# Merging the triangular inverses of two heads in one block, and scaling the heads' outputs on ScalarE, in a bidirectional hybrid encoder layer

## The chip, the cores and the metric

The kernel runs on one core of a Trainium2 chip. The metric is the device time of one execution in microseconds (us), and "the time" of a kernel is the median of its runs. The core has five engines with a queue each: TensorE (PE in the profile; PEld is its weight load), VectorE (DVE), ScalarE (ACT), GpSimd (POOL) and SyncE (SP), which here issues transfers. Products are made by PE and land in PSUM, of which this kernel uses eight banks; all else lies in SBUF or in the chip's main memory.

## What is computed

One encoder layer on 512 positions of 1024 channels in float32: a feed-forward block, a token mixer, a second feed-forward block, a last norm. The change lies in the mixer, in its branch with a delta rule, which has 8 heads, chunks, and one scan per direction:

```python
k_beta = k * beta[..., None]
a_mat = jnp.where(strict, jnp.einsum('bhnid,bhnjd->bhnij', k_beta, k) * decay, 0.0)
a_mat = a_mat + jnp.eye(CHUNK, dtype=q.dtype)
sol = lax.linalg.triangular_solve(a_mat, rhs, left_side=True, lower=True)
...
o = _rmsnorm(o_fwd + o_bwd, dn_norm) * jax.nn.silu(dn_z.reshape(bn, s, DN_HEADS, DN_DV).astype(f32))
```

Instead of a solve the kernel forms the inverse of the unit triangular matrix (chunks of 128 positions, four per direction, so eight matrices of 128x128 for each head) and multiplies by it. The norm of the last line divides each row of a head's 512x128 output by its root mean square.

## The kernel before

Weights stream from main memory in tiles of 128 columns; each is split by ScalarE (`hi`, L219) and VectorE (`lo`, L221) in two halves, and three large products (L231 to L233, 128x128 by 128x512) replace one of full precision. The mixer makes 60 such projections. Between them stands the work of the heads, written as generators that are advanced step by step:

- `build` (`b0` to `b7`): short convolutions, the decays, and the strictly triangular matrices `nl` (L799) and the attention matrices `at` (L803). It transposes through banks tp and kq (L728).
- `invert` (`i0` to `i2`, one for each group of heads (0, 1, 2), (3, 4, 5), (6, 7)): the 32x32 diagonal blocks are inverted on VectorE, a chain of 60 small instructions (L829, L831), and written to main memory (`da`).
- `place` (`p0` to `p7`): four DMAs (L842) bring a head's 32x32 inverses to a pair of buffers `t64[i]` (i is the head's parity), and `merge` joins them in four stages, with a `yield` after each of the first three. Four transposes on VectorE (L851). First stage: 16 products of 32x32 (L858) in two banks, tp and kq, and two copies by ScalarE to `w` (L863). Second: 32 products (L869, L873) in the same two banks and four copies (L877, L879); this gives inverses of 64x64. Third: eight products of 64x64 (L885) in tp and a copy to `w2` (L887). Fourth: eight products (L891, L892) in tp; then VectorE (L905, L909) and GpSimd (L900 to L907) write the inverse with its factors over `nl`, as the factor `f`. A float32 product stands in the trace as two instructions.
- `scan` (`s0` to `s7`): four steps of both directions (products L923, L929, L940; ScalarE copies `y`, L932 and L934; VectorE `yw`, L937), the outputs (L952, L957, L960), then the norm: four squares with a sum on ScalarE (L968), two small VectorE instructions, a power on GpSimd (`rr`, L972), four multiplications by `rr` on VectorE (L974), one for each 128 positions, and four transposes by PE through bank tp (L979).

The order is a list written by hand, `EMIT`: each token advances one generator by one step. `advance` first completes what a step needs: `p` of a head needs `p` two heads earlier (they share `t64`) and its group's inverse; `s` needs `s` two heads earlier and its own `p`. Tokens `z`, `g`, `a`, `m`, `y` are projections and other work that depend on no scan step. From this order a scheduler at compile time makes each engine's fixed queue: among the instructions that it takes to be ready it chooses the earliest emitted. `keep_in_program_order` pins an instruction behind the one emitted before it on its engine; the first two stages' products are pinned, all but the first of each stage. Banks tp, kq and o have one buffer each, and PE's queue is worked in order.

## Time and profile before

| | |
|---|---|
| median of 3 runs | 1325.02 us (1324.39 to 1325.54) |
| profiled execution | 1323.76 us, of it the span 1321.6 us |
| PE busy | 1298.8 us (98%) |
| DVE, ACT, POOL busy | 960.6, 644.9, 64.4 us (73, 49, 5%) |
| mixer's merges and scans | from 540 to 872 us of the span |
| PE, DVE, ACT busy in these 332 us | 324.29, 229.82, 173.77 us |

The page of a profile gives each engine's busy time, the chain of work that ended last, and groups of instructions by line of the kernel. A group's row reads: line, engine, operation, what it writes and reads with sizes, count, busy time, mean nanoseconds of one, and the idle time of the engine just before these with what ended it. A row by line or tile has the minimum, median and maximum of one instruction in ns, and the first and last start. A row of the waits reads: who waited for whom, us in total, times, longest. A row in order of time reads: start, length, engine, line, operation; the ends of PE's products are modelled and overlap, so their starts tell the pace. A row of a stage reads: the stretch, its length, and the busy time of PE, PEld, DVE, ACT and POOL with the number of instructions, then PE's clock, the share of the DMA engines and GB/s.

### The profile page before, as it was taken

What the parts mean: (1) busy time and instruction counts of PE and PEld (TensorE: products, weight loads), DVE (VectorE), ACT (ScalarE), POOL (GpSimd) and SP (SyncE); (2) the same over time, 40 slices, a digit from 0 to 9 for tenths busy, and PEclk for the clock granted to TensorE, in tenths of its full rate; (3) what the DMA queues carried; (4) which work ended last, traced back from release to release, by engine and by line L of the source; (5) the groups of instructions that cost most, each with busy time, mean ns of one, the idle gap of its engine ahead of it and who ended that gap; (6) DMA issues with size and microseconds to landing.
All of it is one profiled execution on the core that took longest, in us unless ns stands there. A gap on an engine that the chain in (4) does not pass through costs nothing.

```text
span 1321.6 us, 22139 instructions
## 1 busy us (share of the span) xinstructions
PE 1298.8 (98%) x8489; PEld 1132.1 (86%) x8489; DVE 960.6 (73%) x1979; ACT 644.9 (49%) x1309; POOL 64.4 (5%) x104
## 2 busy tenths in 40 slices
PE   8999999999999999999999999999999999999997
PEld 7889998888898888787777787888999999998886
DVE  7968886777667889766956785648579888875442
ACT  4445563322357773566464334545446556653330
POOL 0000000000010110112012101000000000000000
PEclk9999999999999999999999999999999999999999
DMA  9433327898433543334333242667423323337421
GB/s 357 172 112 115 109 97 264 288 329 295 145 116 119 164 126 116 119 121 132 128 113 102 76 143 81 190 224 254 160 112 112 112 96 109 115 88 256 126 90 64
DMA packets 83026, 199.91 MB, mean 151 GB/s; under 512 B 25129, under 2 KB 27369, under 8 KB 82666
## 3 DMA queue, kind: packets, MB, share of 16 engines
q1 hardware_dynamic: 64984, 164.29, 37.4%
q10 hardware_dynamic: 17938, 34.23, 7.6%
q8 instruction: 66, 1.08, 0.3%
q14 instruction: 38, 0.31, 0.1%
HBM read 175.39 MB, written 23.10 MB: 150 GB/s over the span
## 4 chain that ended last, share of the span: by engine, by line
PE 82%; issue 9%; DVE 3%; ACT 2%; POOL 2%; DMA 1%; ACTq 0%; POOLq 0%; DVEq 0%; SPq 0%
PE acc L231 16%; PE acc L233 16%; PE acc L232 16%; PE acc L459 12%; PE ch L459 9%; PE acc L1215 1%; PE ch L929 1%; PE ch L1215 1%; PE o L952 1%; PE ch L940 1%; PE ch L957 1%; PE ch L923 1%; PE acc L1043 1%; PE acc L1041 1%; PE acc L1042 1%
## 5 line engine op out<-in xcount | busy, mean ns | idle before, releaser
L231 PE MATMUL acc<-uh,hi 128*128 128x512 f32 (+1 forms) x776 | 297.3, 385 | 0.6 <-DVE sps L644 0.5
L232 PE MATMUL acc<-uh,lo 128*128 128x512 f32 (+1 forms) x776 | 296.4, 383 | 0.1
L233 PE MATMUL acc<-ul,hi 128*128 128x512 f32 (+1 forms) x776 | 295.1, 382 | 0.0
L219 ACT CAST hi<-raw 128x512 fp32r<-128x512 f32 (+1 forms) x276 | 165.9, 612 | 262.9 <-PE acc L233 214.3
L221 DVE TENSOR_TENSOR lo<-raw,hi 128x512 fp32r<-128x512 f32 (+1 forms) x276 | 185.2, 680 | 136.6 <-ACT hi L219 135.0
L231 PEld LDWEIGHTS acc<-uh,hi 128*128 128x128 f32 x776 | 146.1, 189 | 24.8 <-issue 0.7
L232 PEld LDWEIGHTS acc<-uh,lo 128*128 128x128 f32 x776 | 146.0, 188 | 23.4 <-DVE lo L221 0.2
L233 PEld LDWEIGHTS acc<-ul,hi 128*128 128x128 f32 x776 | 145.5, 188 | 23.9
L231 PE MATMUL acc<-g,hi 128*128 128x512 f32 (+1 forms) x396 | 145.0, 366 | 0.0
L232 PE MATMUL acc<-g,lo 128*128 128x512 f32 (+1 forms) x396 | 144.5, 365 | 0.0
L233 PE MATMUL acc<-g,hi 128*128 128x512 f32 (+1 forms) x396 | 144.5, 365 | 0.0
L232 PEld LDWEIGHTS acc<-g,lo 128*128 128x128 f32 x396 | 74.4, 188 | 12.1
L233 PEld LDWEIGHTS acc<-g,hi 128*128 128x128 f32 x396 | 74.4, 188 | 12.0
L231 PEld LDWEIGHTS acc<-g,hi 128*128 128x128 f32 x396 | 74.4, 188 | 12.0
L459 PE MATMUL acc<-dh,hi 128*128 128x256 f32 x368 | 80.2, 282 | 0.0
L691 DVE SCALAR_TENSOR_TENSOR cacc<-acc,cvd_sb,cacc 128x510 f32<-128x510 f32 (+1 forms) x96 | 70.8, 741 | 2.5 <-ACT cacc L686 1.8
L242 DVE TENSOR_TENSOR lw<-raw,hw 128x1024 fp32r<-128x1024 f32 x42 | 51.4, 1224 | 28.8 <-ACT hw L241 28.2
L241 ACT CAST hi<-s 128x512 fp32r<-128x512 f32 x84 | 52.0, 619 | 34.3 <-PE ch L459 14.5
L241 ACT CAST hw<-raw 128x1024 fp32r<-128x1024 f32 x42 | 44.0, 1048 | 48.2 <-PE acc L459 26.7
L459 PE MATMUL acc<-dh,lo 128*128 128x256 f32 x224 | 63.3, 283 | 0.0
L459 PE MATMUL ch<-uh,lw 128*128 128x256 f32 x224 | 62.9, 281 | 0.0
L459 PE MATMUL ch<-ul,hw 128*128 128x256 f32 x224 | 62.8, 281 | 0.0
(385 smaller groups left out, 2812.0 us busy)
## 6 DMA issues: line engine op xcount, KB each, us to landing
raw<-w_in SPq DMA_DIRECT2D x60, 512.0 KB
room<-w_ada SPq DMA_DIRECT2D x40, 512.0 KB
raw<-w2u SPq DMA_DIRECT2D x35, 512.0 KB
raw<-w_ada SPq DMA_DIRECT2D x32, 512.0 KB
raw<-w1u SPq DMA_DIRECT2D x31, 512.0 KB
raw<-w1d SPq DMA_DIRECT2D x12, 512.0 KB
raw<-w2d SPq DMA_DIRECT2D x12, 512.0 KB
rb<-w2u SPq DMA_DIRECT2D x9, 512.0 KB
```

The lines of the kernel that those rows point to most:

```text
L219: act.copy(hi[:], raw[:, k : k + n, :])
L221: last["lo"] = dve.tensor_sub(lo[:], raw[:, k : k + n, :], hi[:].bitcast(F32))
L231: pe.matmul(ps[:, t0:t1], wh, rh[:, k0 + k, t0:t1], start=a, stop=False)
L232: pe.matmul(ps[:, t0:t1], wl, rh[:, k0 + k, t0:t1], start=False, stop=False)
L233: pe.matmul(ps[:, t0:t1], wh, rl[:, k0 + k, t0:t1], start=False, stop=b)
L241: act.copy(hi, src)
L242: dve.tensor_sub(lo, src, hi.bitcast(F32))
L459: pe.matmul(ps, a, b, start=first and k == 0 and a is wh and b is xh, stop=end, skip_group_check=not first)
L691: dve.scalar_tensor_tensor(out=acc[:, lo:hi], in0=src[:, lo + o : hi + o], scalar=w[:, i : i + 1], in1=acc[:, lo:hi], op0=ALU.mult, op1=AL ...
L923: pe.matmul(ps[:, 0:P], kT[:, c * P : c * P + P], S[:], start=True, stop=True)
L929: pe.matmul(ps[:, 0:P], f[:, n, :], r, start=True, stop=True)
L1215: pe.matmul(early[m][:], terms[i][0][:, m, :], terms[i][1], start=k == 0 and i == 0, stop=k == KT - 1 and i == 2)
```

## The change

Heads 0 and 1, 4 and 5, 6 and 7 are merged together; 2 and 3 stay alone. `LEADERS` sends every token of `p0`, `p4`, `p6` to `p1`, `p5`, `p7`, and the followers' tokens drop out of the order, so that a pair's stage stands where the leader's stood. `place` and `merge` take a list of heads. Per stage the products of the lower head come first, then the other's, in the same banks: bank columns 0 to 255 and 256 to 511 in the first, second and fourth stage, and a bank for each head (tp and kq) in the third. All stages' products are now pinned, all but the first of each. The copies keep their sizes and number, one set for each head, and follow all of the stage's products. In the last step VectorE's two multiplications are emitted ahead of GpSimd's. Apart from that, L974's multiplications become ScalarE activations (Copy with a factor for each row).

```diff
+LEADERS = {"p0": "p1", "p4": "p5", "p6": "p7"}
...
-            def place(i, s, da, j):
-                th, tht = t64[i]
-                for b in range(4):
...
-                return merge(s, t64[i])
+            def place(heads):
+
+                for i, s, da, j in heads:
+                    th, _ = t64[i % 2]
+                    for b in range(4):
...
+                return merge([(s, *t64[i % 2]) for i, s, _, _ in heads])
+
+            def pinned_products(todo):
+
+                for n, (out_, a, b) in enumerate(todo):
+                    x = pe.matmul(out_, a, b, start=True, stop=True)
+                    if n:
+                        tc.keep_in_program_order(x)
...
+                ps = [bank("tp", psx), bank("kq", psx)]
+                ws = [one.tile([P, 8, 32], F32, tag="w", bufs=2, name="w") for _ in heads]
+                pinned_products([(ps[b][a0 : a0 + 32, 256 * i + 32 * n : 256 * i + 32 * n + 32],
+                                  nls[i][d0 : d0 + 32, n, a0 : a0 + 32], heads[i][2][d0 : d0 + 32, n, 32:64])
+                                 for i in range(len(heads)) for n in range(8) for b, (a0, d0) in enumerate(halves)])
+                for i, w in enumerate(ws):
+                    for b, (a0, _) in enumerate(halves):
+                        act.copy(w[a0 : a0 + 32].rearrange("p a b -> p (a b)"),
+                                 ps[b][a0 : a0 + 32, 256 * i : 256 * i + 256])
                 yield
...
+                pinned_products(todo)
+                for i, (_, th, tht) in enumerate(heads):
+                    for b, (a0, d0) in enumerate(halves):
+                        o = slice(256 * i, 256 * i + 256)
+                        act.copy(tht[a0 : a0 + 32, :, 32:64], ps[b][a0 : a0 + 32, o].rearrange("p (a b) -> p a b", a=8))
+                        act.copy(th[d0 : d0 + 32, :, 0:32], ps[b][d0 : d0 + 32, o].rearrange("p (a b) -> p a b", a=8))
+                yield
+                ps = [bank(x, psx) for x in ("tp", "kq")[: len(heads)]]
+                pinned_products([(ps[i][0:64, 64 * n : 64 * n + 64], nls[i][64:128, n, 0:64], tht[64:128, n, :])
+                                 for i, (_, _, tht) in enumerate(heads) for n in range(8)])
...
-                for c in range(NC):
-                    dve.tensor_scalar(out=on[:, c, :], in0=on[:, c, :], scalar1=rr[:, 1, c : c + 1],
-                                      scalar2=None, op0=ALU.mult)
+                for c in range(NC):
+                    act.activation(out=on[:, c, :], in_=on[:, c, :], func=ACT.Copy, scale=rr[:, 1, c : c + 1])
...
             def done(t):
+                t = LEADERS.get(t, t)
                 return t in live and live[t] is None
...
-            for t in EMIT + [f"s{i}" for i in range(H)] * 20 + ["z", "g", "a", "m", "y"] * 20:
+            for t in [x for x in EMIT if x not in LEADERS] + [f"s{i}" for i in range(H)] * 20 + ["z", "g", "a", "m", "y"] * 20:
                 advance(t)
```

## The prediction

> **What bounds the kernel now.** I read the page first: its busy row, the slices, the shares of the chain.

> ```profile
> span 1321.6 us, 22139 instructions
> PE 1298.8 (98%) x8489; PEld 1132.1 (86%) x8489; DVE 960.6 (73%) x1979; ACT 644.9 (49%) x1309; POOL 64.4 (5%) x104
> ...
> PEclk9999999999999999999999999999999999999999
> ...
> PE 82%; issue 9%; DVE 3%; ACT 2%; POOL 2%; DMA 1%; ACTq 0%; POOLq 0%; DVEq 0%; SPq 0%
> ```

> TensorE (PE) is busy for 98% of the span at full clock and holds 82% of the chain. Time is therefore won only where PE issues less or stands less; time saved on another engine counts only if PE was waiting for it. The change touches the mixer's stretch in which heads are merged and scanned, so the second view is the busy time by stage, and the third, over the same stretch, whom PE waited for.

> ```profile
> 540.00:600.00 60.00, 57.90 (x575) 47.37 (x573) 44.06 (x140) 42.77 (x126) 11.55 (x19) 1.00 0.32 102
> ...
> 660.00:720.00 60.00, 58.89 (x638) 46.19 (x636) 36.44 (x111) 35.09 (x90) 12.16 (x21) 1.00 0.33 101
> ...
> 800.00:872.00 72.00, 72.00 (x427) 58.57 (x427) 41.83 (x97) 33.80 (x82) 4.05 (x7) 1.00 0.43 139
> ```
> ```profile
> PE tp L979 <- DVE on L974: 3.3, 3, 1.8
> PE ch L940 <- DVE yw L937: 1.6, 2, 0.9
> ...
> PE tp L885 <- ACT t L877: 0.3, 1, 0.3
> ```

> PE (first column after the length) stands for only 2.1, 1.1 and 0.0 us in these stages. Its largest wait is for the scaling of the heads' outputs, 3.3 us; the merge's own waits are small, as L885's 0.3. So the change can gain little by removing waits. What a busy figure hides is how densely PE works while busy, and that is the fourth view: PE's instructions in order of time around small products.

> ```profile
> 671.17 0.39 PE L233 MATMUL acc<-ul,hi 128*128 128x512 f32 x1
> 671.40 0.39 PE L231 MATMUL acc<-uh,hi 128*128 128x512 f32 x1
> 671.72 0.24 PE L858 MATMUL tp<-t,nl 32*32 32x32 f32 x2
> 671.89 0.50 PE L232 MATMUL acc<-uh,lo 128*128 128x512 f32 x1
> 672.23 0.40 PE L233 MATMUL acc<-ul,hi 128*128 128x512 f32 x1
> ...
> 694.22 0.40 PE L232 MATMUL acc<-uh,lo 128*128 128x512 f32 x1
> 694.54 1.14 PE L885 MATMUL tp<-t,nl 64*64 64x64 f32 x16
> 695.62 0.50 PE L233 MATMUL acc<-ul,hi 128*128 128x512 f32 x1
> 695.95 0.39 PE L231 MATMUL acc<-uh,hi 128*128 128x512 f32 x1
> ```

> Read the starts. Large products follow each other at 0.23 us (671.17 to 671.40). Around two tiny 32x32 products the way from one large start (671.40) to the second one after (672.23) is 0.83, where two steps are 0.46: the block costs 0.37 us, nearly all of it going in and out. The 64x64 block goes from 694.22 to 695.95, 1.73 us, less 0.46 is 1.27; its 16 products step by (1.14 - 0.22)/15 = 0.061 us, 0.98 together, so 0.29 is fixed. I take **0.32 us a block**, whatever it holds.

> **The change, part by part.**

> *Fewer blocks.* The stages' arithmetic stays: the same small products, the same copies. What goes is entries and exits of blocks. The first and the last row of such blocks are

> ```profile
> 541.07 0.24 PE L858 MATMUL tp<-t,nl 32*32 32x32 f32 x2
> ...
> 838.24 0.22 PE L892 MATMUL tp<-t,w 64*64 64x64 f32 x1
> ...
> 675.28 0.19 PE L873 MATMUL tp<-t,w 32*32 32x32 f32 x1
> 675.40 0.50 PE L233 MATMUL acc<-ul,hi 128*128 128x512 f32 x1
> 675.83 0.21 PE L869 MATMUL kq<-w,t 32*32 32x32 f32 x1
> ```

> and between them I count 27 blocks of 32x32 and 17 of 64x64. Eight heads of four stages would be 32; the other 12 come of splits, of which the last three rows show one: four products of the second stage, a large product, then the rest, which waited for the second copy of L863. By pairs, in the order of time: heads 1 and 0 have 12 blocks, 5 and 4 have 10, 7 and 6 have 12; heads 2 and 3 alone have 10. The pairs' 34 become 12 at the least (four stages each), and 30 if the second head's products always find their copies late and stay a block of their own and some first products still run ahead. Between these I take 20: the stages stand apart in the order of emission, with projections between them, so most find their copies done, but the pairs that come as soon as they are ready (1 and 0, as now at 541 to 556) will split. That is 14 blocks fewer, 14 x 0.32 = **-4.5 us**; ends -7.0 (22 blocks) and -1.3 (4).

> *Longer copies between the stages.* The group view gives the copies:

> ```profile
> L863 ACT COPY w<-kq 32x256 f32<-32x256 f32 x8 | 2.9, 363 | 0.2
> ...
> L877 ACT COPY t<-kq 32x256 f32<-32x256 f32 x8 | 2.9, 363 | 0.2
> ...
> L887 ACT COPY w<-tp 64x512 f32<-64x512 f32 x8 | 4.6, 579 | 9.5 <-PE tp L885 6.3 <-PE ch L929 3.3
> ...
> L905 DVE TENSOR_TENSOR nl<-tp,st 64x256 f32<-64x256 f32 x8 | 3.3, 413 | 7.7 <-PE tp L892 7.7
> ...
> L906 POOL TENSOR_TENSOR nl<-t,st 64x256 f32<-64x256 f32 x8 | 4.8, 605 | 0.0
> ```

> A pair's first stage is followed by four copies instead of two, the second by eight instead of four, 8 x 0.363 = 2.9 us, the third by two of 0.579. PE's queue is in order, so a product of the next stage that stands too early stops the projections behind it, as L885 did for 0.3. I allow two more such waits, **+0.7 us**. The ends: none; and the whole second set of four copies, 1.45 us, in each of three pairs, +4.4. GpSimd (POOL) has eight products of 0.605 for a pair where it had four, so the scan of head 1, which is emitted ahead of head 0's, finds its factor 2.4 us later. I cost that at nothing: projections cover it, which stand between the scan's steps; without them it would be 2.4 us once for each pair. The follower's four DMAs and four transposes move ahead with the leader's. On SP four more issues of 0.445 us then stand ahead of weight loads, and on VectorE (DVE) four more transposes of 0.434 us ahead of the weights' `lo` halves. Rows for both:

> ```profile
> L842 SPq DMA_DIRECT2D t<-da x32: 303/445/501, 537.1 to 789.2; - x32
> ...
> L851 DVE STREAM_TRANSPOSE t<-t 32x256 f32<-32x256 f32 x32 | 13.9, 434 | 1.7 <-DMA t<-da 1.0
> L219 ACT CAST hi<-raw 128x512 fp32r<-128x512 f32 x74 | 45.8, 618 | 61.9 <-PE acc L233 51.3 <-PE acc L1043 4.7 <-issue 2.6
> ```

> Their cover is the last row: the weights' casts wait 51.3 us for PE to free a buffer and none in the row for a load, so weights lie ready before PE wants them. I cost both at nothing; without that cover it is 1.8 us a pair (4 x 0.445).

> *The factor on ScalarE (ACT).* 32 multiplications leave DVE and become ACT instructions.

> ```profile
> L974 DVE TENSOR_SCALAR on<-on,rr 128x128 f32<-128x128 f32 x32 | 9.6, 344 | 8.4 <-POOL rr L972 8.4
> L974 DVE TENSOR_SCALAR on<-on,rr x32: 270/280/1269, 597.3 to 870.8; 128x128 f32<-128x128 f32 x32
> ...
> L934 ACT ACTIVATE y<-ch,st 128x128 f32<-128x128 f32 x32 | 11.7, 366 | 18.3 <-PE ch L929 18.2
> L968 ACT ACTIVATE junk<-on 128x128 f32<-128x128 f32 x32 | 9.8, 308 | 4.6 <-DVE on L960 4.1
> ```
> ```profile
> 734.30 1.01 POOL L972 TENSOR_TENSOR rr<-rr,mhalf 128x4 f32<-128x4 f32 x1 [15.94 <-DVE rr L970]
> 735.27 1.26 POOL L822 TENSOR_SCALAR_AFFINE_SELECT A<-A 64x1024 f32<-64x1024 f32 x1
> ...
> 735.34 1.27 DVE L974 TENSOR_SCALAR on<-on,rr 128x128 f32<-128x128 f32 x1 [1.13 <-POOL rr L972]
> ```

> DVE is rid of 9.6 us of work and 8.4 us of standing in line for POOL's 1.0 us power. ACT gets 32 x 0.308 to 0.366, 9.9 to 11.7 us (I take 0.366, the same function with a factor per row), and stands in line instead. Behind it wait the copies `y` of whichever scan runs alongside, hence `yw` and L940, and the weights' casts, which have the cover named above. The rows at 735 show what else goes: a DVE multiplication took 1.27 us, where the median is 0.28, while a POOL instruction ran exactly alongside, and PE's 1.8 us wait is there. On ACT it would be 0.37, so that wait shrinks by 0.9; the two others depend on POOL's power and stay. **-1.0 us**. Ends: -4.9, if all of L974's 3.3 and `yw`'s 1.6 go; and +3.2, if the four links take ACT 4 x (0.366 - 0.270) = 0.4 us longer than DVE and PE waits for that in all eight heads.

> [...]

> **Sum.** -4.5 + 0.7 - 1.0 = -4.8 us. The profiled execution took 1323.76 us, 2.2 of them outside its span; it becomes 1319.0. It lies 1.26 below the median of the three runs, 1325.02, and by that I set **1320.2 us**. All bounds together: -7.0 - 4.9 = -11.9 gives 1313.1, and -1.3 + 4.4 + 3.2 = +6.3 gives 1331.3.

> **The rivals.**

> *The blocks do not merge* (it does not do what it says). The pins hold a block's products only in their order: anything ready goes between. For: the split at 675.40, and copies of 0.36 to 0.58 us per head and quadrant that the second head must await. Against: stages that are emitted apart now run in one block. Then -1.3 + 0.7 - 1.0 = -1.6: 1323.4, no measurable change.

> *ACT's queue takes over DVE's wait.* Eight waits of about 1.05 us (8.4/8) move in front of `y`; if PE pays half, +4.2, against -4.8: 1324.4. For: L934 and the casts are in that queue. Against: ACT has the lower load in all three stages, and DVE, which the scan needs twice per step, is freed.

> *Slower: a pair holds its two PSUM banks too long.* Banks tp and kq have one buffer each, and the transposes of `build` and of the outputs and the products at L794 need them. Per pair one unbroken hold grows by 0.73 us (first stage), 1.45 (second), 0.98 + 0.58 (third, which now has both banks) and 0.83 (fourth): 4.6, three pairs 13.7. It decides once PE stands for over 4.8/13.7, a third of it; at two thirds it is +9.1 - 4.8 = +4.3: 1329.3. For: PE's order is fixed beforehand. Against: the total of holds per head is unchanged, and projections fill. [...]

> *Faster than forecast:* 12 blocks left and the two DVE waits gone, near 1314.

> **How the numbers follow.** 0.2%, about what a measurement of this kernel can tell from no change, is 2.65 us. Forecast 0.50; no merging 0.14; ACT's queue 0.10; banks 0.18; faster still 0.08. The forecast's own range, 1316 to 1323, lies nearly all beyond 2.65 us, the two neutral cases nearly all within. Faster 0.58, same 0.24, slower 0.18. The range for 8 in 10 goes from 1314.0 to 1328.0.

> **What would show it.** Right: some 30 blocks of small products instead of 44, 64-product blocks of L858's stage and 128-product ones of the next; L979's wait at about 2 us; DVE less by 9 to 10 us and ACT more by 10 to 12. Wrong, by the rivals: still 40 blocks; PE waits on ACT `y` or `yw` above 4 us; PE waits at the transposes or L794 above 6 us in the three pairs' stretches.

## The result and the profile after

The kernel after takes 1329.86 us (median of 5 runs, 1328.9 to 1331.85) against 1325.02 (5 runs, 1324.39 to 1326.28): a ratio of 1.0035, 95% interval 1.0024 to 1.0045. It is 4.8 us slower where 4.8 us faster was forecast, and lies outside the range. The profiled execution took 1331.48 us, of it the span 1329.3, 7.7 more than before. Where the clock is said below to be halved or not, it is the one profiled execution of that kernel. Two far longer executions below (2618.7 us with pair 5/4 alone, 1893.14 us with the shorter run on POOL) count in those kernels' medians and not in their ratios.

First the page's busy row, then the stages that the prediction quoted, in the same columns.

```profile
span 1329.3 us, 22126 instructions
...
PE 1303.3 (98%) x8489; PEld 1134.5 (85%) x8489; DVE 955.5 (72%) x1947; ACT 655.2 (49%) x1341; POOL 64.8 (5%) x104
...
PEclk9999999999999999999998999999999999999999
```
```profile
540.00:600.00 60.00, 57.65 (x557) 46.30 (x555) 45.27 (x134) 37.26 (x100) 9.71 (x17) 0.97 0.37 112
660.00:720.00 60.00, 56.01 (x617) 44.87 (x616) 34.83 (x100) 34.06 (x89) 11.54 (x19) 0.94 0.31 95
800.00:872.00 72.00, 71.58 (x573) 57.73 (x572) 41.83 (x90) 36.21 (x87) 6.85 (x11) 1.00 0.40 132
```

Two things are new. PE stands for 4.0 us from 660 to 720, where it was 1.1. And the granted clock, 1.00 throughout the mixer before, is 0.97 and 0.94 in the first two stages: in the page's row of slices one digit is 8. The trace has the clock at 0.50 for 3.4 us from 565.9 and for 6.8 us from 709.2. Counted by the large products (3,376 in both traces, in the same order), this kernel is 0.1 us behind the old one at 540, 2.5 at 660, 7.0 at 720, 7.3 at 872 and 7.8 at the end. Most of the loss comes by 720, where the pairs 1/0 and 5/4 are done; behind that 0.8 us more is lost and nothing won back.

The waits of PE in the mixer (us in total, times, longest):

```profile
PE tp L853 <- ACT w L897: 3.1, 2, 2.8
PE tp L993 <- ACT on L989: 1.9, 3, 0.7
PE ch L943 <- ACT y L946: 1.1, 1, 1.1
...
PE kq L796 <- ACT vt L732: 0.9, 1, 0.9
PE ch L943 <- DVE nl L915: 0.7, 1, 0.7
```

L993 is the old L979: its wait for the scaled outputs fell from 3.3 to 1.9 us, as forecast. The first row is the merge itself. L853 are all of its small products, and the product that waits 2.8 us is the first of the second head in pair 5/4's fourth stage. Why it waits is read in three queues. PE first (start, length):

```profile
704.51 1.14 PE L853 MATMUL tp<-t,nl 64*64 64x64 f32 x16
705.49 1.09 PE L853 MATMUL kq<-t,nl 64*64 64x64 f32 x16
...
707.75 0.40 PE L234 MATMUL acc<-uh,lo 128*128 128x512 f32 x1
710.98 0.36 PE L853 MATMUL tp<-w,t 64*64 64x64 f32 x1 [2.84 <-ACT w L897]
...
712.79 0.78 PE L235 MATMUL acc<-ul,hi 128*128 128x512 f32 x1
```

Both heads' third stage is done by 706.6, in banks tp and kq. Then ACT:

```profile
706.17 0.58 ACT L897 COPY w<-tp 64x512 f32<-64x512 f32 x1
710.06 0.40 ACT L989 ACTIVATE on<-on,rr 128x128 f32<-128x128 f32 x1 [3.31 <-POOL rr L986]
710.37 0.56 ACT L897 COPY w<-kq 64x512 f32<-64x512 f32 x1
```

ACT copies the first head's `w2`. Next in its queue is a scaling (L989), which is not ready; ACT stands 3.31 us before it, and the second head's copy, whose input has been there since 706.6, comes behind. What L989 waits for is POOL's:

```profile
702.27 0.92 POOL L918 TENSOR_TENSOR nl<-t,st 64x256 f32<-64x256 f32 x1 [2.38 <-ACT t L888]
...
707.82 0.62 POOL L922 TENSOR_TENSOR nl<-t,st 64x256 f32<-64x256 f32 x1
708.37 0.56 POOL L917 MEMSET nl<- 64x256 f32 x2
709.01 1.01 POOL L986 TENSOR_TENSOR rr<-rr,mhalf 128x4 f32<-128x4 f32 x1
```

The power of the norm (L986) stands behind the pair's eight multiplications, 702.3 to 708.4, and two memsets. Its input comes from DVE:

```profile
706.62 0.57 DVE L984 SCALAR_TENSOR_TENSOR rr<-rr 128x4 f32<-128x4 f32 x1
```

It is there at 707.2, so POOL's queue adds 1.8 us. The rest of ACT's 3.31 us is the time until that input is there and the 1.0 us of the power itself. At the other seven norms the power starts at most 0.15 us after its input. So ACT's order holds PE, and here POOL's run makes the hold longer. The last quoted row of PE shows what follows: a large product takes 0.78 where it took 0.39. The same 4-us slices of the stage view give the clock (the number behind POOL's busy time):

```profile
708.00:712.00 4.00, 1.16 (x17) 0.93 (x16) 0.00 (x0) 1.76 (x5) 1.94 (x4) 0.66 0.44 132
712.00:716.00 4.00, 4.00 (x18) 3.69 (x17) 2.04 (x5) 0.85 (x2) 0.00 (x0) 0.50 0.00 0
716.00:720.00 4.00, 4.00 (x28) 3.25 (x27) 0.70 (x2) 3.46 (x18) 0.00 (x0) 0.99 0.00 0
```

The half clock begins at 709.2, while PE stands, and goes on until 716.1, 5.1 us after PE works again. From 712 to 716 PE counts as fully busy at half its clock. No view of busy time or of waits shows that; only the clock's column does.

### The profile page after: what moved, and what is told of

Its sections match the earlier page's. It is cut to its first block, busy times and chain, and to the rows that moved or that the text cites. A ratio compares the mean times of both kernels' runs of the same rounds, so it can differ in the third digit from the quotient of the medians.

```text
span 1329.3 us, 22126 instructions
## 1 busy us (share of the span) xinstructions
PE 1303.3 (98%) x8489; PEld 1134.5 (85%) x8489; DVE 955.5 (72%) x1947; ACT 655.2 (49%) x1341; POOL 64.8 (5%) x104
## 4 chain that ended last, share of the span: by engine, by line
PE 84%; DVE 5%; ACT 4%; issue 3%; DMA 2%; POOL 1%; POOLq 0%; DVEq 0%; SPq 0%; ACTq 0%
PE acc L235 17%; PE acc L233 17%; PE acc L234 17%; PE acc L461 12%; PE ch L461 9%; PE acc L1233 1%; PE ch L943 1%; PE ch L1233 1%; PE tp L853 1%; ACT hi L221 1%; PE o L966 1%; PE ch L954 1%; ACT junk L735 1%; DVE lo L223 1%; PE acc L1055 1%
## 5 line engine op out<-in xcount | busy, mean ns | idle before, releaser
L233 PE MATMUL acc<-uh,hi 128*128 128x512 f32 (+1 forms) x776 | 298.4, 386 | 0.7 <-DVE sps L646 0.5
L233 PEld LDWEIGHTS acc<-uh,hi 128*128 128x128 f32 x776 | 146.1, 189 | 25.1 <-issue 0.7
L233 PE MATMUL acc<-g,hi 128*128 128x512 f32 (+1 forms) x396 | 144.9, 366 | 0.0
L233 PEld LDWEIGHTS acc<-g,hi 128*128 128x128 f32 x396 | 74.4, 188 | 12.1
```

Source lines behind the costliest of these rows:

```text
L233: pe.matmul(ps[:, t0:t1], wh, rh[:, k0 + k, t0:t1], start=a, stop=False)
```

## The experiments

The theory after this reading: the two parts of the change hurt each other. Merging puts POOL's multiplications in one run of eight, the scaling makes ACT wait for the power behind them, and the merge's copies stand behind the scaling. The rivals: one part is bad by itself; the pair's hold of the banks (the prediction's slower case); or the half clock, whatever starts it. The ratios are to the kernel before, run on the same chip, with 95% intervals. The kernel before had medians of 1326.26 to 1326.99 us there, so a ratio can lie below 1 where the median lies above 1325.02.

**Each part alone.** Merging without the scaling on ACT (kernel after, L989 undone):

```diff
-                    act.activation(out=on[:, c, :], in_=on[:, c, :], func=ACT.Copy, scale=rr[:, 1, c : c + 1])
+                    dve.tensor_scalar(out=on[:, c, :], in0=on[:, c, :], scalar1=rr[:, 1, c : c + 1],
+                                      scalar2=None, op0=ALU.mult)
```

> The merged pairs, with the multiplications back on VectorE. Theory Q (queues): in the changed kernel the scaling of head 2's output stands on ScalarE in front of the pair 5/4's second w2 copy and waits for GpSimd's power, which stands behind the pair's eight multiplications; TensorE waits 2.8 us for that copy and is then granted half its clock for 6.8 us. With the scaling on VectorE the copy is not held up: L897's wait under 0.5 us, no half clock near 709 us, time 1324 to 1326. Theory B (banks: a pair holds tp and kq too long, whatever engine scales): both stay, 1329 to 1331.

Measured: 1325.88 us, ratio 0.9996 (0.9986 to 1.0005). The wait for `w2` is gone, and no half clock in the mixer.

The scaling on ACT without merging (kernel before, the same lines the other way):

> The kernel before with only the scaling moved to ScalarE. Q: GpSimd's run ahead of the power is four multiplications and not eight, so no wait of TensorE over 1.5 us and no half clock; time 1323 to 1326. Rival (the move itself costs, because the y copies stand behind it): TensorE's waits on y or yw over 4 us, time 1328 or more. B: as before, 1325.

Measured: 1323.24 us, ratio 0.9976 (0.9967 to 0.9986). So neither part is bad alone; the scaling gains 0.24%, merging nothing, and together they lose 0.35%. The parts interact. These kernels do not differ in the edited lines alone, since each edit lets the scheduler set new orders: the traces of the kernel after and of the one that only merges differ in the place of some 800 of PE's 8,489 instructions. The next edit leaves the orders nearly as they were.

**The order in ACT's queue alone.** The scaling is kept behind the copies of `w2` emitted last:

```diff
-                    act.copy(w2s[-1][:].rearrange("p a b -> p (a b)"), x[0:64, :])
+                    last["w2"] = act.copy(w2s[-1][:].rearrange("p a b -> p (a b)"), x[0:64, :])
...
-                for c in range(NC):
+                with tc.issue_after(last["w2"].ins):
+                  for c in range(NC):
```

> The changed kernel with the scaling queued on ScalarE behind the last emitted w2 copy; on ScalarE only one instruction changes its place. Q: the wait of 2.8 us and the half clock behind it go, 1329.9 - 2.8 - 2.0 = 1325 (1324 to 1326). B and the rival of a general reshuffle: 1329 to 1330.

Measured: 1326.45 us, ratio 0.9998 (0.9987 to 1.001), no half clock in the mixer. In the traces the queues of DVE and POOL are those of the kernel after, instruction by instruction. ACT's differs in one place, the second `w2` copy of pair 5/4 ahead of the scaling; PE's differs in a few products between 707 and 728 us. All work is the same, and the same instructions take and free each bank; the loss is gone with the order. The row of this kernel's waits that replaced it:

```profile
PE kq L796 <- ACT vt L732: 2.7, 2, 1.8
PE tp L993 <- ACT on L989: 1.8, 3, 0.7
```

Another copy of ACT is now the late one: ACT still stands 2.82 us before the scaling, with `vt` behind it.

**Does the standing bring the half clock?** Thirteen unused products of 128x128 fill the place where PE stood:

```diff
-                        todo += [(ps[0:64, o], th[0:64, c, :], w2s[i][:, c, :]),
+                        todo += [(ps[:, 256:384], ident[:], ones[:])] * (13 * (c == 0 and s is S[5])) + [(ps[0:64, o], th[0:64, c, :], w2s[i][:, c, :]),
```

> The changed kernel with 13 dummy products (128x128, some 2.9 us of TensorE) between the two heads' products of the pair 5/4's fourth stage, where it stood for 2.8 us; the wait itself stays. If the half clock after the wait is a cost of TensorE standing, it goes and the time falls by 2 to 2.5 us to about 1327.5. If the half clock has another cause, or costs nothing, the time stays at 1330 or rises by up to 0.5.

Measured: 1329.31 us, ratio 1.0028 (1.0016 to 1.004). The half clock was still there, from 707.8 to 711.2, 3.4 us instead of 6.8. As a test of the standing it failed: PE had already stood elsewhere in the 3.4 us before. That is seen in its order of time:

```profile
704.07 0.40 PE L233 MATMUL acc<-uh,hi 128*128 128x512 f32 x1
705.46 0.39 PE L234 MATMUL acc<-uh,lo 128*128 128x512 f32 x1 [0.99 <-issue]
```

**One pair at a time**, with the scaling on ACT. `LEADERS` keeps one entry: `{"p0": "p1"}`, `{"p4": "p5"}` or `{"p6": "p7"}`.

> Only heads 0 and 1 are merged; the scaling is on ScalarE. By Q the pair saves five blocks (1.6 us) and pays about as much in waits near 563 us (ScalarE's vt copy, the factor's write): the ratio to the kernel before is that of the scaling alone, 0.9976, within 0.001. By B each pair pays for its banks: 1.000 or more.

> Only heads 4 and 5 are merged; the scaling is on ScalarE. By Q this pair carries the long wait for a w2 copy behind head 2's scaling: a wait of TensorE on ACT w of 2 us or more, and a ratio of 0.9976 + 0.003 = 1.000 to 1.002. If the schedule falls out so that the scaling stands behind the copy, no such wait and 0.997. By B the same as the other pairs.

> Only heads 6 and 7 are merged; the scaling is on ScalarE. By Q four blocks fewer (1.3 us) and no long wait: ratio 0.9976 - 0.001 = 0.9966. By B as the other pairs, 1.000 or more.

Measured: pair 1/0 alone 1330.81 us, ratio 1.0036 (1.0024 to 1.0049); pair 5/4 alone 1331.31, 1.0036 (1.0023 to 1.0049); pair 7/6 alone 1324.97, 0.999 (0.998 to 1.0001). All three lie above what was expected. That pair 1/0 alone costs as much as all three was the furthest off, and the place was still less expected: its half clock lies at 711.2 to 721.4, by heads 5 and 4, which are not merged there. The order of ACT's queue in that stretch shows the same jam, now before the copies of the second stage:

```profile
708.56 0.40 ACT L989 ACTIVATE on<-on,rr 128x128 f32<-128x128 f32 x1 [1.63 <-POOL rr L986]
708.87 0.34 ACT L888 COPY t<-tp 32x256 f32<-32x256 f32 x1
709.24 0.36 ACT L889 COPY t<-tp 32x256 f32<-32x256 f32 x1
```

PE waited 1.6 us for L889 there. In the kernel with pair 5/4 alone ACT stood 2.96 us, with all four scalings ahead of the copies, and PE waited 1.8:

```profile
699.14 1.28 ACT L989 ACTIVATE on<-on,rr 128x128 f32<-128x128 f32 x4 [2.96 <-POOL rr L986]
700.45 0.36 ACT L888 COPY t<-tp 32x256 f32<-32x256 f32 x1
```

In neither kernel was POOL's run the cause; POOL was idle when the power's input came, as in the kernel with pair 1/0 alone:

```profile
707.10 1.43 POOL L986 TENSOR_TENSOR rr<-rr,mhalf 128x4 f32<-128x4 f32 x1 [1.30 <-DVE rr L984]
```

So neither the length of a merged block nor POOL's run is needed for such a jam: in these three kernels a copy that PE is about to need stands behind a scaling whose factor is not made yet. That place follows from the whole order, which each of these edits changes.

**A shorter run on POOL alone.** Four of a pair's eight multiplications go to DVE:

```diff
-                    pool.tensor_tensor(out=f[0:64, NC:8, 0:64], in0=th[0:64, NC:8, :], in1=sc(rki, 0), op=ALU.mult)
-                    pool.tensor_tensor(out=f[64:128, NC:8, 64:128], in0=th[64:128, NC:8, :], in1=sc(rki, 64),
+                    dve.tensor_tensor(out=f[0:64, NC:8, 0:64], in0=th[0:64, NC:8, :], in1=sc(rki, 0), op=ALU.mult)
+                    dve.tensor_tensor(out=f[64:128, NC:8, 64:128], in0=th[64:128, NC:8, :], in1=sc(rki, 64),
                                       op=ALU.mult)
```

> The changed kernel with two of a head's four multiplications of the factor on VectorE instead of GpSimd, so that GpSimd's run of a pair is four long and not eight. By Q head 2's power is no longer late, the w2 copy is held up by under 0.5 us, and no half clock follows: 1325 to 1326.5. By B 1329 to 1331.

Measured: 1325.48 us, ratio 0.999 (0.9979 to 1.0002). The `w2` wait is gone, and the power starts 0.1 us after its input, but ACT still stands 2.20 us before a scaling with the second stage's copies behind it, PE waits 1.46 us for L889, and its profile has the clock at half for 10.2 us from 708.0:

```profile
703.30 1.28 ACT L989 ACTIVATE on<-on,rr 128x128 f32<-128x128 f32 x4 [2.20 <-POOL rr L986]
704.60 0.36 ACT L888 COPY t<-tp 32x256 f32<-32x256 f32 x1
```

**Order and shorter run together.** The last edit and that of ACT's order:

> Merged pairs and scaling on ScalarE as in the kernel after, with both repairs: the scaling stands behind the w2 copies in ScalarE's queue, and GpSimd has four multiplications of a pair instead of eight (VectorE has the other four). Theory: the change's own waits are gone, the blocks saved (3.5 us) and the shorter wait for the outputs (1.4 us) remain, so at a granted clock of 0.998 the kernel takes some 1321 us, 3 below the kernel before; each half-clock stretch of 3.4 us that it draws costs 1.7 us at most, so its median lies at 1321 to 1325. Rival (the two repairs mend the same wait, and merging itself gains nothing): 1324 to 1326, no better than either repair alone. The ScalarE w wait should be below 0.5 us.

Measured: 1319.87 us (1319.38 to 1320.92), ratio 0.9951 (0.9937 to 0.9964), no half clock in the mixer, granted clock 0.997 or 0.998 in all five runs. That is below the 1321 to 1325 expected. It beats both kernels, and every large wait is gone:

```profile
PE tp L993 <- ACT on L989: 0.9, 2, 0.6
PE ch L971 <- ACT y L946: 0.8, 1, 0.8
PE ch L943 <- DVE nl L915: 0.6, 1, 0.6
PE tp L853 <- ACT t L889: 0.6, 2, 0.3
```

Pair 5/4 in its ACT queue, to be laid beside the rows at 706 to 710 above:

```profile
706.22 0.58 ACT L897 COPY w<-tp 64x512 f32<-64x512 f32 x1
...
706.72 0.58 ACT L897 COPY w<-kq 64x512 f32<-64x512 f32 x1
707.20 1.28 ACT L989 ACTIVATE on<-on,rr 128x128 f32<-128x128 f32 x4
```

The scaling follows the copies and does not wait: the power was done at 701.8.

Here too hardly anything else moved. Against the kernel with the shorter run alone, the queues of PE, DVE and POOL are the same instruction by instruction, and in ACT's only four instructions have moved, the scaling of head 2 from ahead of pair 5/4's copies to behind them. With that PE's 1.46 us before L889 and the half clock of 10.2 us went, and the median fell from 1325.48 to 1319.87. At an equal granted clock of 0.997 the runs took 1322.4 (one) and 1319.9 (two), which leaves 2.5 us at equal clock.

**What of that is the shorter run?** Two more cells: the shorter run and the scaling on ACT without merging, and the shorter run and merging with the scaling on DVE.

> The kernel before (no merged pairs) with scaling on ScalarE and with two of GpSimd's four multiplications per head on VectorE. It tells what in the half-GpSimd kernel's gain belongs to merging: if merging adds nothing, this is as fast as that kernel at equal clock (some 1321.5 us at 0.998) or faster, and draws fewer half-clock stretches, so a median of 1321 to 1323; if the gain came from merging's fewer blocks, this stays where scaling alone was, 1323.2 or above.

> Merged pairs, the scaling on VectorE as in the kernel before, and four of a pair's eight multiplications of GpSimd on VectorE. With the runs so far this fills the last cell: merging with the long GpSimd run and scaling on VectorE was 1325.9, no change. Theory (GpSimd's run of eight eats what the fewer blocks save, whoever does the scaling): with a run of four, the 3.5 us of the blocks show, and the time is 1322 to 1323.5. Rival (the gain of the kernel with both repairs needs ScalarE's scaling): VectorE, which now has the scaling and four more multiplications for each pair, is late with yw and the factor, and the time stays at 1325 to 1328.

Measured: without merging 1331.87 us, ratio 1.0044 (1.003 to 1.0059); with the scaling on DVE 1325.09, 0.9983 (0.9973 to 0.9992). The multiplications on DVE are at most a small gain by themselves. Without merging the time is 8 us above that of the scaling alone, which neither side had expected, PE waits for DVE instead, and its profile has the half clock for 3.4 us from 609.8:

```profile
PE ch L940 <- DVE yw L937: 2.0, 3, 1.4
...
PE o L952 <- DVE at L803: 1.7, 2, 1.1
PE tp L869 <- DVE z L984: 1.6, 1, 1.6
```

With the scaling on DVE as well, `on` and `yw` are late, and the half clock follows a wait for `yw` (3.4 us from 623.3):

```profile
PE tp L993 <- DVE on L988: 3.5, 3, 1.7
PE ch L954 <- DVE yw L951: 2.1, 2, 1.9
```

The theory that POOL's run alone eats what merging saves fell; the rival, that the gain needs the scaling on ACT, fits. What the shorter run itself is worth stays open, since moving it also set new orders: some 1,900 of PE's instructions stand elsewhere than in the kernel after, and without merging some 2,600 elsewhere than with the scaling alone. The cells in one table (median in us; ratio to the kernel before on the same chip, so compare cells by the ratio):

| scaling on | multiplications on POOL, ACT's order | not merged | merged |
|---|---|---|---|
| DVE | all | 1325.02; 1 | 1325.88; 0.9996 |
| DVE | half | | 1325.09; 0.9983 |
| ACT | all | 1323.24; 0.9976 | 1329.86; 1.0035 |
| ACT | all, behind `w2` | | 1326.45; 0.9998 |
| ACT | half | 1331.87; 1.0044 | 1325.48; 0.999 |
| ACT | half, behind `w2` | | 1319.87; 0.9951 |

**Do crowded small products halve the clock without standing?** In the kernel after, 64 unused products of 64x64 stand in a row in pair 7/6's fourth stage; in a second kernel each eight of them are followed by 13 products of 128x128:

```diff
+                        todo += [(ps[0:64, 256:320], th[0:64, 0, :], w2s[0][:, 0, :])] * (64 * (c == 0 and s is S[6])) + ...
```

> The kernel after with 64 extra products of 64x64, unused, one after the other ahead of the second head's products in the fourth stage of heads 7 and 6. At 0.061 us an instruction, 128 instructions, they take 7.8 us in which TensorE never stands. Theory A (the clock is set by how much full-sized work a window of 3.41 us holds): at least one whole window holds small products alone, so the clock is halved there in every run, for 3.4 to 6.8 us, and the kernel takes 8 to 13 us more than the kernel after. Theory B (only standing halves the clock): no half clock there, and 7.8 us more.

> The same 64 small products in eight blocks of eight, each followed by 13 unused products of 128x128 (some 0.7 us), so that no window of 3.41 us holds small products alone; the share of full-sized work is about a third throughout. Theory A: no half clock there; the time is the kernel after's plus 7.8, plus 8 x 0.7 for the large ones and up to 8 x 0.32 for going in and out, 13 to 16 us in all. If the clock is halved here as well, theory A's share is wrong or its limit lies above a third.

Measured: 1338.02 us, 8.2 above the kernel after (6.9 by the ratios), ratio 1.0087 (1.0067 to 1.0108), and 1360.29, ratio 1.0255 (1.0234 to 1.0277). The second costs twice the estimate because I had priced 13 float32 products of 128x128 at 0.7 us; they are 26 instructions and take 3.1. The crowd's own row, and the clock over it:

```profile
811.66 7.51 PE L853 MATMUL tp<-w,t 64*64 64x64 f32 x126
```
```profile
812.00:816.00 4.00, 4.00 (x72) 4.00 (x71) 0.40 (x1) 0.43 (x1) 0.00 (x0) 1.00 0.42 131
816.00:820.00 4.00, 4.00 (x88) 4.00 (x85) 0.00 (x0) 0.00 (x0) 0.00 (x0) 1.00 0.02 4
```

7.5 us of small products alone leave the clock at 1.00. Theory A fell. Theory B, that it takes standing (1.0 to 2.8 us in the step ahead of each half clock of the mixer, see the last section), fits all traces: in the two edits of ACT's order alone (the kernel after against the ordered one, and the shorter run against both repairs) less standing and no half clock came together.

## Why the prediction was wrong

**Fewer blocks: the count right, the price not.** 44 blocks became 33, by the same count in the trace; the forecast was 30. The pairs' 34 became 21 (20 forecast), while heads 2 and 3 went from 10 to 12. At 0.32 us that would be -3.5 instead of -4.5. PE's busy time does not show it. Merged kernels without a half clock in the mixer have 1298.1 us (scaling on DVE), 1298.2 (ordered scaling) and 1298.9 (both repairs), with 10 or 11 blocks fewer, against 1298.8 before. The ordered kernel's row:

```profile
PE 1298.2 (98%) x8489; PEld 1130.3 (85%) x8489; DVE 955.7 (72%) x1947; ACT 654.9 (49%) x1341; POOL 65.0 (5%) x104
```

So at most 0.7 us of the 3.5 came. The price was read around single blocks among large products, and the sum over the kernel was not held against it; where the rest went stays open. The rival "the blocks do not merge" is out by the count, though its time, no measurable change, is what merging alone gave.

**The scaling: right, and larger than said.** L993's wait fell to 1.9 us (about 2 forecast), ACT gained 10.3 us of busy time (10 to 12 forecast). DVE lost 5.1 instead of 9 to 10, which was not followed up. Alone the scaling gained 0.24%, 3.2 us, where -1.0 stood in the sum (its working, 1.27 less 0.37, gives -0.9), with -4.9 as its end. Four scalings in a row on ACT took 1.28 us (the x4 rows of L989 above), 0.32 each, where 0.366 was taken; one by itself took 0.40, at 710.06.

**The step that failed.** Two terms failed. The smaller is the price of a block, above. The larger is in "longer copies between the stages": the waits of PE on the merge's copies, "two more such waits, +0.7 us". I took those copies to start as soon as their products are done. With the scaling on ACT they also stand behind it in ACT's queue, and it waits for a factor that is not made yet. Before, L974 waited for the power on DVE, 8.4 us in all, and PE paid 3.3 of them. Now the groups of instructions have ACT standing there 11.4 us:

```profile
L989 ACT ACTIVATE on<-on,rr 128x128 f32<-128x128 f32 x32 | 10.8, 392 | 11.5 <-POOL rr L986 11.4
```

The waits on `w2` were 3.1 us in place of 0.7, and then came the half clock, which the prediction did not consider, because before it the mixer's clock was 1.00 throughout. POOL's eight multiplications for a pair, "I cost that at nothing", made it worse: I followed them only to the factor of head 1's scan and not to the power, which stands in the same queue. That is 1.8 of the 11.4 us, all at the one norm that falls into pair 5/4's merge. The rival "ACT's queue takes over DVE's wait" had the right engine and a chance of 0.10, but the wrong thing behind it: `y` (1.1 us, one wait) and the casts, not the merge's own copies.

The half clock at pair 1/0 has nothing to do with a scaling. It follows waits of 0.9 us (L796 for `vt`) and 0.7 (L943 for the factor), and the ordered kernel has the same two waits and kept its clock there (see the last section).

The terms, as far as they can be set: of the 7.7 us by which the spans differ, PE stands for 3.2 (26.0 against 22.8) and is busy for 4.5. The half clock's 10.2 us lose an estimated 4.1 by the slope below, nearly all of the 4.5; that leaves nothing for the blocks. The profiled run has a lower clock (0.994) than its kernel's median run (0.995).

**Banks held too long: not it.** With the scaling ordered, and the same products and copies in the same banks, the time is back at the old one. The bank waits that there are in the kernel after (L796 behind `vt`, 0.9 us) are small.

The forecast time, 1320.2, is nearly that of the kernel with both repairs, 1319.87. That is chance. It is another kernel, on a chip where the kernel before took 1326.34 (at an equal clock of 0.998 the gain is 4.3 us, 1324.6 to 1320.3), and its profile gains by other terms: PE's waits from 400 to 960 add up to 5.9 us instead of 8.1, and its busy time is the old one. Half of the multiplications are no longer on POOL and the scaling is ordered, and why the same move of multiplications costs so much without merging (1331.87) was not settled.

## What to carry to other kernels

Before an instruction is given to an engine, list for each of its inputs what stands ahead of the producer in the producer's queue, and for the instruction itself what stands behind it in its new queue: a wait that was cheap on one engine is dear where PE's inputs stand behind it (here 8.4 us on DVE, of which PE paid 3.3; 11.4 on ACT, where PE waited 3.1 for the copies and 6.8 us at half clock came with it). Two edits that each gain or do nothing must be followed through the queue that they share: here one puts both heads' copies one behind the other on ACT and the other puts a waiting scaling ahead of them. A price read around one instruction should be held against the engine's busy time over the whole kernel (here 3.5 us by the price, at most 0.7 in PE's busy time). Read the clock's column where PE stands between small products: here it stood for 1.0 to 2.8 us in the step of 3.41 ahead of each half clock of the mixer, and in the kernel after it then counts as busy for 4.00 of 4.00 us at a clock of 0.50 (712 to 716).

## What the runs showed of the hardware

The spread between runs of one kernel goes for the most part with the clock. Of the 88 runs of the kernel before beside the experiments, the 13 with a granted clock of 0.998 took 1324.6 us on average, the 31 with 0.996 took 1326.7, the 5 with 0.994 took 1328.6; the clock accounts for two thirds of the variance. Fitted over the runs of all kernels, each about its kernel's mean, a microsecond of clock lost (the time multiplied by one minus the granted clock) costs an estimated 0.8 us. At 0.996 the kernel after took 1329.2 (2 runs): 2.5 us of its loss remain at equal clock, and the rest goes with its lower clock (0.995 on average against 0.996).
